# A streaming-encoder block in split float32: seven products for twelve units of the down product, sums and gate multiplications queued elsewhere, and smaller moves at the beginning and the tail

## The chip, the cores and the metric

One core of a Trainium2 chip runs the whole block in one launch. The metric is the device time in microseconds (us), the median of repeated runs. The engines are named as in the profile: PE (TensorE, matmuls and transposes), PEld (its weight loads), DVE (VectorE), ACT (ScalarE), POOL (GpSimd) and SP (SyncE, which issues nearly all DMAs). A trace comes from one profiled execution; its span runs from the first to the last instruction.

## What is computed

One layer on a batch of 256 tokens of 2048 channels in float32, with 256 memory tokens:

```python
def swiglu(h, w_gate, w_up, w_down):
    return (jax.nn.silu(h @ w_gate) * (h @ w_up)) @ w_down

x = x + 0.5 * swiglu(rms_norm(x, ffn1_norm), ffn1_w_gate, ffn1_w_up, ffn1_w_down)
h = rms_norm(x, mix_norm)
u, q, k, v, g, a_lr = split(h @ w_in)
x = x + concatenate([pool_mixer(u), gla_mixer(q, k, v, g, a_lr)]) @ w_out
x = x + mem_cross_attention(rms_norm(x, xattn_norm), rms_norm(mem, mem_norm), w_q, w_kv, w_o)
x = x + 0.5 * swiglu(rms_norm(x, ffn2_norm), ffn2_w_gate, ffn2_w_up, ffn2_w_down)
out = rms_norm(x, final_norm)
```

The hidden width of both FFNs is 5632, eleven pieces of 512. The pool mixer has four channel groups with trailing means; the GLA mixer is gated linear attention with four heads in chunks of 64 tokens.

## The kernel before

**Numbers.** Every float32 operand is split into a high part and a low part of the type fp32r: the high part is a cast (ACT, `wh`, `xh`, line 228), the low part a subtraction (DVE, `wl`, `xl`, line 229). A product is three matmuls: high by high, high by low, low by high (`products`, which ends in line 307).

**Units.** The weights come in units of 1 MB, two k-tiles of 128 rows by 1024 columns. A unit is loaded by SP (`raw`, three buffers, three units ahead), split into `wh` and `wl` (three buffers; two units ahead, one ahead for the first four) and used by 24 matmuls of 128x512 in `block_t` (line 307): 2 k-tiles x 2 halves of the columns (j) x 2 halves of the tokens (h) x 3. `block_a` and `block_b` are other forms for `w_in`, `w_kv` and such.

**Seven products.** In `block_s` (gate and up, lines 401 to 460) the units of `PAIRS` (0, 2, 4) are done by Winograd's form of Strassen's scheme: the 2x2 block product (2 token halves by 2 k-tiles, 2 k-tiles by 2 column halves) takes seven block products for eight, 21 matmuls for 24. It needs sums of the weight blocks (`add_weights`, lines 363, 366 and 367, into `T`), split again (`wh<-T`, `wl<-T`, and `xh`, `xl` for the three blocks used as they are), sums of the activations (`part_sums`, into `xe`, lines 346 to 357), and at the end sums of the PSUM banks (`combine`, lines 443 to 448, into `sg`; `join`, line 452). Two PSUM tiles, `parts`, take four of the seven products, two others, `ps`, the result itself.

**Order.** `Stream` collects units and operations. `st.op(f, after=n)` puts an operation behind n more units; the program order that this gives is then arranged by a scheduler, which fixes one order for each engine. PSUM has four tiles of two banks, handed out as they come free.

**FFN.** The hidden pieces come in three parts, `FF_PARTS = ((0, 4), (4, 4), (8, 3))`. In each part, gate and up of two pieces at a time: `ev_gate` applies SiLU with the row factor `Rcol` (line 676, ACT), `ev_up` multiplies by up and `Rcol` (line 681, DVE, into `sg`), `turn` transposes the result on PE (line 691, `ph`) and splits it into `ys` (lines 234 and 235). The third part ends with one piece whose gate and up make one block. Then the down product (`into_x`, two column blocks b of `block_t`) adds to x by `residual` (line 608). Both down products of the third part and all other products into x keep this form; the last one of FFN 2 is `down_end`.

**Beginning.** `turn_gains` transposes a tile of the norms' gains (line 539, `pgain`), `x_chunk` transposes x by PE (line 575, `px`), scales it by the gains and splits it into `xs` (lines 210 and 211); `x_squares` and `finish_norm` make `Rcol` (lines 186 to 198) while the first gate runs, since the row factor is applied to its results.

**Mixer.** `pool_unit` makes four groups (`pp`, line 805) that `pool_out` evicts; `scores` and `attend` (`po`, line 954) handle the four GLA heads, in two pairs b, behind the units of v.

**Tail.** In `down_end` the last unit of every column block leaves its second token half for `second_half`: x is updated (line 1188), squared (line 1191), the row factor made (lines 1196 and 186 to 198), and eight output pieces multiplied (lines 1203 to 1209) and written (line 1210).

Of the kernel before, what the change touches and what calls it, by code (L numbers as in the profile page):

```python
# [14 lines left out]
P = 128  # L15
D = 2048
# [76 lines left out]
def build(ctx, tc, I, out):  # L93
# [87 lines left out]


# [43 lines left out]

    def split_weights(hi, lo, src):
        in_turn("scalar", lambda: nc.scalar.copy(hi, src))  # L228
        in_turn("vector", lambda: nc.vector.tensor_tensor(  # L229
            out=lo, in0=src, in1=f32(hi), op=ALU.subtract  # L230
        ))
# [8 lines left out]
    def row_squares(src, c):  # L240

        for h in range(2):
            j = tmp.tile([P, S], F32, tag="j", name=uid("j"), bufs=2)
            nc.scalar.activation(j, src[h], AF.Square, accum_out=ss[:, h, c : c + 1])
# [96 lines left out]
    def part_sums(act, ext, i, g):  # L341

        t = scope["pool"].tile([P, 4 * NB], F32, tag="T", name=uid("T"))
        a = t[:, :NB].rearrange("p (k s) -> p k s", k=2)
        e = t[:, NB : 2 * NB].rearrange("p (n s) -> p n s", n=4)
        nc.vector.tensor_tensor(
            out=a, in0=f32(act[:, 2 * g : 2 * g + 2, 0, :]), in1=f32(act[:, 2 * g : 2 * g + 2, 1, :]),
            op=ALU.add,
        )
        a11, a21, a12, a22 = (a[:, k, h * P : (h + 1) * P] for k in range(2) for h in range(2))  # L350
        nc.vector.tensor_tensor(out=e[:, 3], in0=a11, in1=a21, op=ALU.subtract)
# [33 lines left out]
    def seven(banks, act, ext, i, g, first, later, weights):  # L385
# [3 lines left out]
        n4, n1, s2, s3 = ([ext[:, i, p, n] for p in range(2)] for n in range(4))  # L389
# [6 lines left out]
        order = ("P1", "P7", "P5", "P6", "P2", "P3", "P4") if first else (  # L396
            "P1", "P2", "P3", "P7", "P5", "P6", "P4")
        for n in order:
            (a, b), wh, wl = table[n]
            for j, (x, w) in enumerate(((a, wh), (a, wl), (b, wh))):  # L400
                nc.tensor.matmul(  # L401
                    banks[n], x, w, start=first and j == 0,
                    stop=not later and n in ("P1", "P5", "P6", "P7") and j == 2,
                )

    def block_s(srcs, act, ext, pairs, evict, delays=(0, 0)):

        held, n = {}, len(srcs)

        def open_banks():  # L410
            a, b, c, d = (ptile(uid("pt")) for _ in range(4))
            held["ps"] = (d, c)
            held["parts"] = (a, b)
            held["banks"] = {
                "P1": a[:, 0], "P6": a[:, 1], "P7": b[:, 0], "P5": b[:, 1],
                "P2": c[:, 0], "P4": c[:, 1], "P3": d[:, 0],
            }

        def unit_s(g):
            def fn(weights):  # L420
                if g == pairs[0]:
                    open_banks()
                seven(held["banks"], act, ext, pairs.index(g), g, g == pairs[0], g != pairs[-1],
                      weights)
            return fn

        def unit_p(g):
            def fn(wh, wl):
                wh, wl = (w.rearrange("p (k j n) -> p k j n", j=2, n=NB) for w in (wh, wl))
                for j in (1, 0):  # L430
                    for h in range(2):
                        for kk in range(2):

                            fresh = (j, h) == (0, 1) and g == min(set(range(n)) - set(pairs)) and kk == 0
                            products(held["ps"][j][:, h, :], act, 2 * g + kk, h, wh[:, kk, j],
                                     wl[:, kk, j], fresh, g == n - 1 and kk == 1)
            return fn

        def combine():
# [8 lines left out]
            nc.vector.tensor_tensor(out=e[:, 3], in0=b[:, 1], in1=e[:, 1], op=ALU.add)  # L448

        def join(j):  # L450
            e = held["e"][:, 0:2] if j else held["e"][:, 2:4]
# [5 lines left out]
        for g, src in enumerate(srcs):  # L457
            if g in pairs:
                st.unit(src, unit_s(g), split_seven, add_weights)
                if g == pairs[-1]:  # L460
                    st.op(combine)
            else:
                st.unit(src, unit_p(g))
        for j in (1, 0):
            st.op(lambda j=j: join(j), delays[j])
# [65 lines left out]
    def gain_columns(names, queue):  # L531
        t = rows["gain"] = scope["pool"].tile([P, P], F32, tag="gain", name=uid("gain"), bufs=2)
        nc.vector.memset(t, 0.0)
# [3 lines left out]
    def turn_gains(lo, hi):  # L537
        ps = ptile(uid("pgain"))
        nc.tensor.transpose(ps[:, 0, :P], rows["gain"], ident)
        nc.vector.tensor_copy(gains[:, lo:hi], ps[:, 0, lo:hi])  # L540
# [63 lines left out]
    def residual(scale, b):  # L604

        def evict(j, ps):
# [4 lines left out]
            if j:  # L611
                store_x(b)
        return evict

    def fold(c, gain):
# [10 lines left out]
        for h in range(2):  # L626
            q = tmp.tile([P, NB], F32, tag="j", name=uid("j"), bufs=2)
            nc.scalar.activation(q, x[:, h], AF.Square, accum_out=ss[:, h, c : c + 1])

    def into_x(w, act, scale, gain=None, k0=0, nk=KT, spread_too=True, src=None):  # L630

        for b in range(2):
            st.op(lambda b=b: fetch_x(b, src), 2)
            block_t(wwide(w, b * 2 * NB, k0, nk), act, residual(scale, b))
# [10 lines left out]
    PAIRS = (0, 2, 4)  # L645

    def pair_sums(g, delay):
        def f():
            if g == PAIRS[0]:
                rows["xe"] = scope["pool"].tile(  # L650
# [659 lines left out]
```

## Time and profile before

| | us |
|---|---|
| median of 3 runs | 2133.31 (2133.0 to 2134.68) |
| profiled execution | 2133.11 |
| its span | 2131.2 |
| PE busy | 2111.3 |
| DVE busy | 1427.7 |
| ACT busy | 1008.0 |
| matmuls and transposes on PE | 10032 |
| mean TensorE clock granted | 0.999 of full |

The page of the profile has a part with busy time by engine, one with the span in 40 slices, the DMA queues, the chain of work that ended last (followed back from the last instruction), and the costliest groups of instructions. In a group's row stands: line, engine, operation, output <- inputs by the program's names, shape, count | busy time, mean ns of one | idle time of the engine ahead of them and what ended it. The chain can be cut to a window; its rows are start, length, and what. A timeline's rows are start, busy time and the instruction, with the engine's idle time before it in brackets. The view of stretches gives for each stretch its length and the busy time (and instructions) of PE, PEld, DVE, ACT and POOL, then the clock, the busy share of the DMA engines and GB/s.

### The profile page before, as it was taken

How to read it: one execution, taken by the hardware profiler on the slowest of the kernel's cores; microseconds unless marked ns; L12 is line 12 of the kernel's file. 1: busy time of each engine (PE TensorE's matmuls, PEld its weight loads, DVE VectorE, ACT ScalarE, POOL GpSimd, SP SyncE). 2: the span in 40 equal slices, each digit the busy share in tenths (PEclk: the TensorE clock that was granted, in tenths of full speed). 3: DMA queues.
4: the chain of work that ended last, by engine and by line, in shares of the span. 5: the costliest groups of instructions: out<-in, count | busy, mean ns of one | idle time of the engine just before them, and what ended most of it. 6: DMA issues, size and time to landing. Idle time of an engine off the chain costs nothing.

```text
span 2131.2 us, 24070 instructions
## 1 busy us (share of the span) xinstructions
PE 2111.3 (99%) x10032; PEld 1768.5 (83%) x10032; DVE 1427.7 (67%) x1189; ACT 1008.0 (47%) x890; POOL 14.2 (1%) x41
## 2 busy tenths in 40 slices
PE   9999999999999999999999999999999999999998
PEld 7878888888888888888888888888888888888886
DVE  8876588856864576565666454567874888658744
ACT  7554354534534545455445443445443455434433
POOL 0000000000000000000000000000000000000001
PEclk9999999999999999999999999999999999999999
DMA  7556665566656655557654555666576665766663
GB/s 277 197 189 234 224 221 195 186 233 226 227 178 234 221 162 180 167 185 278 222 190 161 167 169 171 195 207 207 175 247 217 214 209 175 249 212 223 221 217 119
DMA packets 143316, 435.91 MB, mean 205 GB/s; under 512 B 9828, under 2 KB 13000, under 8 KB 142824
## 3 DMA queue, kind: packets, MB, share of 16 engines
q1 hardware_dynamic: 143176, 434.38, 60.5%
q8 instruction: 78, 1.28, 0.2%
q14 instruction: 30, 0.25, 0.0%
q10 hardware_dynamic: 32, 0.01, 0.0%
HBM read 417.58 MB, written 16.78 MB: 204 GB/s over the span
## 4 chain that ended last, share of the span: by engine, by line
PE 98%; DVE 1%; issue 0%; ACT 0%; DMA 0%; SPq 0%; DVEq 0%; ACTq 0%
PE pt L307 58%; PE pa L292 15%; PE pt L401 12%; PE pb L307 6%; PE pe L307 3%; PE ph L691 1%; PE pl L1084 1%; PE pv L1119 1%; PE px L621 0%; DVE wl L229 0%; ACT wh L228 0%; DMA x<-in_x 0%; PE px L575 0%; PE po L954 0%; PE pa L832 0%
## 5 line engine op out<-in xcount | busy, mean ns | idle before, releaser
L229 DVE TENSOR_TENSOR wl<-raw,wh 128x2048 fp32r<-128x2048 f32 (+2 forms) x328 | 740.2, 2258 | 544.5 <-ACT wh L228 543.9
L228 ACT CAST wh<-raw 128x2048 fp32r<-128x2048 f32 (+2 forms) x328 | 618.5, 1886 | 721.7 <-PE pt L307 490.5
L307 PE MATMUL pt<-wh,xs 128*128 128x512 f32 x1952 | 618.6, 390 | 0.0
L307 PE MATMUL pt<-wh,ys 128*128 128x512 f32 x1728 | 534.7, 389 | 0.0
L307 PEld LDWEIGHTS pt<-wh,xs 128*128 128x128 f32 x1952 | 366.6, 188 | 75.7
L307 PE MATMUL pt<-wl,xs 128*128 128x512 f32 x976 | 380.8, 390 | 0.0
L307 PEld LDWEIGHTS pt<-wh,ys 128*128 128x128 f32 x1728 | 324.1, 188 | 67.0
L307 PE MATMUL pt<-wl,ys 128*128 128x512 f32 x864 | 336.3, 389 | 0.0
L292 PE MATMUL pa<-xs,wh 128*128 128x512 f32 x896 | 317.1, 398 | 2.1 <-DVE t L266 1.7
L292 PE MATMUL pa<-xs,wl 128*128 128x256 f32 x896 | 248.8, 281 | 0.0
L307 PEld LDWEIGHTS pt<-wl,xs 128*128 128x128 f32 x976 | 183.5, 188 | 37.9
L292 PEld LDWEIGHTS pa<-xs,wh 128*128 128x128 f32 x896 | 167.7, 188 | 41.2 <-issue 2.0
L307 PEld LDWEIGHTS pt<-wl,ys 128*128 128x128 f32 x864 | 162.2, 188 | 33.5
L292 PEld LDWEIGHTS pa<-xs,wl 128*128 128x128 f32 x896 | 169.2, 189 | 1.6 <-issue 0.2
L228 ACT CAST wh<-T 128x2048 fp32r<-128x2048 f32 x54 | 103.3, 1912 | 135.6 <-DVE T L367 93.3
L229 DVE TENSOR_TENSOR wl<-T,wh 128x2048 fp32r<-128x2048 f32 x54 | 123.6, 2288 | 65.3 <-ACT wh L228 65.3
L307 PE MATMUL pb<-wh,xs 128*128 128x512 f32 x384 | 121.7, 392 | 0.5 <-DVE ys L211 0.5
L401 PE MATMUL pt<-wh,xe 128*128 128x512 f32 x324 | 108.7, 389 | 0.0
L229 DVE TENSOR_TENSOR xl<-raw,xh 128x1536 fp32r<-128x1536 f32 x54 | 94.5, 1750 | 2.7 <-ACT xh L228 2.7
L228 ACT CAST xh<-raw 128x1536 fp32r<-128x1536 f32 x54 | 79.9, 1479 | 28.9 <-PE pt L401 28.8
L307 PEld LDWEIGHTS pb<-wh,xs 128*128 128x128 f32 x384 | 72.0, 188 | 15.6 <-DVE ys L211 0.7
L401 PE MATMUL pt<-xh,xs 128*128 128x512 f32 x216 | 78.6, 389 | 1.7 <-DVE sg L452 1.7
(203 smaller groups left out, 1666.3 us busy)
## 6 DMA issues: line engine op xcount, KB each, us to landing
raw<-in_ffn_w_down SPq DMA_DIRECT2D x88, 1024.0 KB, 5.5
raw<-in_ffn_w_up SPq DMA_DIRECT2D x80, 1024.0 KB, 5.0
raw<-in_ffn_w_gate SPq DMA_DIRECT2D x77, 1024.0 KB, 5.0
raw<-in_w_in SPq DMA_DIRECT2D x32, 1024.0 KB, 5.2
raw<-in_xattn_w_kv SPq DMA_DIRECT2D x32, 1024.0 KB, 5.2
raw<-in_w_out SPq DMA_DIRECT2D x16, 1024.0 KB, 6.2
raw<-in_xattn_w_q SPq DMA_DIRECT2D x16, 1024.0 KB, 5.2
raw<-in_xattn_w_o SPq DMA_DIRECT2D x16, 1024.0 KB, 5.6
```

Of the source, the lines that this page charges most:

```text
L228: in_turn("scalar", lambda: nc.scalar.copy(hi, src))
L229: in_turn("vector", lambda: nc.vector.tensor_tensor(out=lo, in0=src, in1=f32(hi), op=ALU.subtract))
L292: nc.tensor.matmul(o, w, x, start=k == 0 and i == 0, stop=last and i == 1)
L307: nc.tensor.matmul(ps, a, w, start=first and i == 0, stop=last and i == 2)
L401: nc.tensor.matmul(banks[n], x, w, start=first and j == 0, stop=not later and n in ("P1", "P5", "P6", "P7") and j == 2,)
L691: nc.tensor.transpose(v[:, i, h * P : (h + 1) * P], g[:, h, i * P : (i + 1) * P], ident)
L1084: nc.tensor.matmul(ps[:, t, :M], ys[:, 4 * h + d, a, tok], xa["K"][:, d, b, :], start=i == 0, stop=i == 11,)
L1119: nc.tensor.matmul(ps[:, d, :S], xa["V"][:, m, a, col], xa["PT"][:, m, b, :], start=i == 0, stop=i == 5,)
```

## The change

1. **Down products of the parts 0 and 1** (both FFNs): `into_x` uses `block_s` for them. In the first column block unit 0 is a seven-product unit, in the second units 0 and 4, in the orders of `Y_ORDER`. `block_s` can take its units in any order, opens the banks of the four part products at the first seven-product unit, and adds the combined parts to x in `merge` as soon as they are there, the whole banks at the end (`residual`).
2. **Sums** of activations become a class. For `ys` (`over`) the fourth sum takes the place of the block of `ys` that no product needs; the others go to a tile `ye`. The temporary is one shared tile of 128x512, `j`.
3. **Gate multiplications** (`late_up`) are queued two units later, or at once ahead of a down product, and behind the latest weight splits (`behind_weights`); turns two or three units later than before in some places.
4. **Sums of FFN 1's activations**: points 5, 6, 7 in place of 5, 5, 5; FFN 2's: 5, 6, 7 in place of 3, 4, 5.
5. **Beginning**: twelve spare transposes, 16 rows of gains transposed rather than 128 with a memset, x chunks 3 to 7 one unit earlier.
6. **Mixer**: two pool groups share one PSUM tile; scores and what follows for the second pair of heads one unit earlier.
7. **Tail**: all matmuls ahead of the row factors, an order of evictions written out, row factor 0 interleaved with the first update, output pieces in halves.

The diff, cut to its core:

```diff
+    def spare_transposes(n):
+        ps = ptile(uid("pwarm"))
+        for _ in range(n):
+            nc.tensor.transpose(ps[:, 0, :P], ident, ident)
...
+    def behind_weights(f):
+        with tc.issue_after(latest["vector"].ins), tc.issue_after(latest["scalar"].ins):
+            f()
...
-    def part_sums(act, ext, i, g):
-        t = scope["pool"].tile([P, 4 * NB], F32, tag="T", name=uid("T"))
-        a = t[:, :NB].rearrange("p (k s) -> p k s", k=2)
-        e = t[:, NB : 2 * NB].rearrange("p (n s) -> p n s", n=4)
-        nc.vector.tensor_tensor(
-            out=a, in0=f32(act[:, 2 * g : 2 * g + 2, 0, :]), in1=f32(act[:, 2 * g : 2 * g + 2, 1, :]),
-            op=ALU.add,
-        )
-        a11, a21, a12, a22 = (a[:, k, h * P : (h + 1) * P] for k in range(2) for h in range(2))
-        nc.vector.tensor_tensor(out=e[:, 3], in0=a11, in1=a21, op=ALU.subtract)
-        nc.vector.tensor_tensor(out=e[:, 1], in0=a22, in1=a21, op=ALU.subtract)
-        nc.vector.scalar_tensor_tensor(
-            out=e[:, 2], in0=e[:, 1], scalar=-1.0, in1=a11, op0=ALU.mult, op1=ALU.subtract
-        )
-        nc.vector.tensor_tensor(out=e[:, 0], in0=a12, in1=e[:, 2], op=ALU.add)
-        split(ext[:, i, 0], ext[:, i, 1], e)
+    def jtile():
+        return tmp.tile([P, NB], F32, tag="j", name=uid("j"))
+    class Sums:
+        def __init__(self, name, act, pairs, over):
+            self.name, self.act, self.pairs, self.over = name, act, pairs, over
+        def make(self, g):
+            act, i = self.act, self.pairs.index(g)
+            n = 3 if self.over else 4
+            if i == 0:
+                self.tile = scope["pool"].tile(
+                    [P, len(self.pairs), 2, n, P], F32R, tag=self.name, name=uid(self.name)
+                )
+            a, k = jtile(), slice(2 * g, 2 * g + 2)
+            nc.vector.tensor_tensor(
+                out=a.rearrange("p (k s) -> p k s", k=2), in0=f32(act[:, k, 0, :]),
+                in1=f32(act[:, k, 1, :]), op=ALU.add,
+            )
+            a = a.rearrange("p (n s) -> p n s", n=4)
+            p11, p21, p12, p22 = (a[:, m] for m in range(4))
+            nc.vector.tensor_tensor(out=p11, in0=p11, in1=p21, op=ALU.subtract)
+            nc.vector.tensor_tensor(out=p21, in0=p22, in1=p21, op=ALU.subtract)
+            nc.vector.scalar_tensor_tensor(
+                out=p22, in0=p11, scalar=-1.0, in1=p22, op0=ALU.mult, op1=ALU.subtract
+            )
+            nc.vector.tensor_tensor(out=p12, in0=p12, in1=p22, op=ALU.add)
+            split(self.tile[:, i, 0], self.tile[:, i, 1], a[:, 4 - n :])
+            if self.over:
+                split(act[:, 2 * g, 0, P:], act[:, 2 * g, 1, P:], p11)
+        def parts(self, g):
+            i, n = self.pairs.index(g), 3 if self.over else 4
+            t = [[self.tile[:, i, p, m] for p in range(2)] for m in range(n)]
+            return [[self.act[:, 2 * g, p, P:] for p in range(2)]] + t if self.over else t
...
-    def block_s(srcs, act, ext, pairs, evict, delays=(0, 0)):
-        held, n = {}, len(srcs)
-        def open_banks():
-            a, b, c, d = (ptile(uid("pt")) for _ in range(4))
-            held["ps"] = (d, c)
-            held["parts"] = (a, b)
-            held["banks"] = {
-                "P1": a[:, 0], "P6": a[:, 1], "P7": b[:, 0], "P5": b[:, 1],
-                "P2": c[:, 0], "P4": c[:, 1], "P3": d[:, 0],
-            }
+    def block_s(srcs, act, sums, order, evict, merge=None, sevens=None):
+        sevens = [g for g in order if g in (sevens or sums.pairs)]
+        held, seen = {"banks": {}}, set()
+        def banks(*names):
+            t = ptile(uid("pt"))
+            for i, n in enumerate(names):
+                held["banks"][n] = t[:, i]
+            return t
+        def open_whole():
+            if "ps" not in held:
+                c = banks("P2", "P4")
+                held["ps"] = (banks("P3", "P0"), c)
+        def open_parts():
+            held["parts"] = (banks("P1", "P6"), banks("P7", "P5"))
...
+            if merge is not None:
+                merge(e[:, 2:4], e[:, 0:2])
         def join(j):
+            if merge is not None:
+                evict(j, held["ps"][j])
...
-        for g, src in enumerate(srcs):
+        for g in order:
+            if g in sevens:
+                st.unit(srcs[g], unit_s(g), split_seven, add_weights)
...
     def turn_gains(lo, hi):
         ps = ptile(uid("pgain"))
-        nc.tensor.transpose(ps[:, 0, :P], rows["gain"], ident)
-        nc.vector.tensor_copy(gains[:, lo:hi], ps[:, 0, lo:hi])
+        n = hi if lo == 0 else P
+        nc.tensor.transpose(ps[:, 0, :n], rows["gain"][:n, :], ident[:n, :n])
+        copied = nc.vector.tensor_copy(gains[:, lo:hi], ps[:, 0, lo:hi])
+        if lo == 0:
+            latest["vector"] = copied
...
+    def early_parts(scale, b):
+        def merge(minus, plus):
+            for j, e, s in ((1, plus, scale), (0, minus, -scale)):
+                x = x_cols((2 * b + j) * NB, NB)
+                nc.vector.scalar_tensor_tensor(
+                    out=x, in0=e, scalar=s, in1=x, op0=ALU.mult, op1=ALU.add
+                )
+        return merge
...
+            if sums is None:
+                block_t(cols, act, residual(scale, b))
+            else:
+                block_s(cols, act, sums, Y_ORDER[b], residual(scale, b, 0), early_parts(scale, b),
+                        Y_SEVEN[b])
...
+    PAIRS, Y_PAIRS = (0, 2, 4), (0, 4)
+    Y_ORDER = ((1, 2, 3, 4, 0, 5, 6, 7), (1, 2, 0, 3, 4, 5, 6, 7))
+    Y_SEVEN = ((0,), (0, 4))
+    CLEAR = PAIRS[-1] + 2
...
+        def late_up(held, j, c):
+            behind_weights(lambda: ev_up(j, c, held))
...
+        for i, g in enumerate(PAIRS):
+            st.op(lambda g=g: x_sums.make(g), 5 + i)
         for lo, n in FF_PARTS:
+            whole = n == KT // 4
...
+                held, up = {}, {}
+                into_down = whole and b
+                block_s(wwide(wu, n0), xs, x_sums, range(8), up.__setitem__)
                 st.op(lambda held=held: held.update(gate))
-                wait = PAIRS[-1] + 2 if b + 2 < n - 1 else 1
+                for j in (1, 0):
+                    st.op(lambda j=j, held=held, up=up: late_up(held, j, up[j]),
+                          0 if into_down else 2)
+                wait = CLEAR if b + 2 < n - 1 else 1 if into_down else 4
...
+            if whole:
+                for g, after in zip(Y_PAIRS, (2, 4)):
+                    st.op(lambda g=g: behind_weights(lambda: y_sums.make(g)), after)
+            down(wd, 4 * lo, 4 * n, lo + n == FF // NB, y_sums if whole else None)
+    st.op(lambda: spare_transposes(12))
     st.op(lambda: turn_gains(0, G_MIX))
-    for c in range(8):
-        st.op(lambda c=c: x_chunk(c), c - 1)
+    st.op(lambda: x_chunk(0))
+    for c in range(1, 8):
+        st.op(lambda c=c: x_chunk(c), c - 1 if c < 3 else c - 2)
...
-    for g in PAIRS:
-        pair_sums(g, 5)
...
-            ps = ptile(uid("pp"))
+            if g % 2 == 0:
+                two = ptile(uid("pp"))
+            ps = two[:, g % 2, :].rearrange("p (a b) -> p a b", a=2)
...
-            st.op(lambda h=h: scores(h), 1 + i)
-            st.op(lambda h=h: attend(h), 2 + i)
-            st.op(lambda h=h: head_squares(h), 2 + i)
+            at = 1 + i - b
+            st.op(lambda h=h: scores(h), at)
+            st.op(lambda h=h: attend(h), at + 1)
+            st.op(lambda h=h: head_squares(h), at + 1)
...
         def second_half():
-            row_factor(0)
-            finish(0, 0, nc.scalar)
-            finish(0, 3)
-            mm(0, nk - 2, 1, *kept[0])
-            finish(0, 1, nc.scalar)
-            finish(0, 2)
-            mm(1, nk - 2, 1, *kept[1])
+            act, dve, half = nc.scalar, nc.vector, NB // 2
+            for b in range(2):
+                mm(b, nk - 2, 1, *kept[b])
+            row_factor(0, lambda: in_order(update(0, 1)))
+            in_order(square(0, 1))
+            weigh(0, 1)
+            finish(act, 0, 0)
+            in_order(update(1, 1))
+            in_order(square(1, 1))
+            weigh(1, 1)
+            finish(act, 0, 1, 0, half)
+            in_order(update(2, 1))
+            in_order(square(2, 1))
+            in_order(update(3, 1))
+            in_order(square(3, 1))
+            finish(dve, 0, 2)
+            finish(dve, 0, 3, 0, half)
+            finish(act, 0, 1, half, NB)
             row_factor(1)
-            for c in range(4):
-                finish(1, c, nc.scalar if c == 1 else None)
+            finish(dve, 1, 2)
+            finish(act, 1, 0)
+            finish(dve, 1, 3)
+            finish(act, 1, 1)
+            finish(dve, 0, 3, half, NB)
...
-    for n, g in enumerate(PAIRS):
-        pair_sums(g, 3 + n)
```

More of the change, by code (lines that the diff above doesn't have):

```diff
@@ L383, in split_seven, with seven @@
         return [parts], None
-    def seven(banks, act, ext, i, g, first, later, weights):
+    def seven(banks, act, sums, g, fresh, ends, weights):
         th, tl, rh, rl = weights
@@ L388, in seven @@
         a11, a12, a22 = ([act[:, k, p, t] for p in range(2)] for k, t in ((k0, lo), (k1, lo), (k1, hi)))
-        n4, n1, s2, s3 = ([ext[:, i, p, n] for p in range(2)] for n in range(4))
+        s3, n1, n4, s2 = sums.parts(g)
         table = {
@@ L431, in fn @@
                     for h in range(2):
+                        n = names[j, h]
                         for kk in range(2):
-                            fresh = (j, h) == (0, 1) and g == min(set(range(n)) - set(pairs)) and kk == 0
-                            products(held["ps"][j][:, h, :], act, 2 * g + kk, h, wh[:, kk, j],
-                                     wl[:, kk, j], fresh, g == n - 1 and kk == 1)
+                            products(held["banks"][n], act, 2 * g + kk, h, wh[:, kk, j],
+                                     wl[:, kk, j], n not in seen and kk == 0,
+                                     g == order[-1] and kk == 1)
+                        seen.add(n)
             return fn
@@ L1145, in last_gain, with down_last @@
         nc.sync.dma_start(fin["gB"], I["final_norm"].partition_broadcast(P))
-    def down_last(wd, k0, nk, last):
+    def down_last(wd, k0, nk, last, sums):
         if last:
@@ L1150, in down_last @@
         else:
[L1151 removed]
+            into_x(wd, ys, 0.5, None, k0, nk, sums=sums)
     def down_end(wd, k0, nk):
```

146 lines of the change are left out of this document (80 added, 66 removed).

## The prediction, made before the result was known

> **What bounds the kernel now.** I read the page first: the busy shares, then the chain that ended last.
>
> ```profile
> span 2131.2 us, 24070 instructions
> PE 2111.3 (99%) x10032; PEld 1768.5 (83%) x10032; DVE 1427.7 (67%) x1189; ACT 1008.0 (47%) x890; POOL 14.2 (1%) x41
> PE 98%; DVE 1%; issue 0%; ACT 0%; DMA 0%; SPq 0%; DVEq 0%; ACTq 0%
> L307 PE MATMUL pt<-wh,ys 128*128 128x512 f32 x1728 | 534.7, 389 | 0.0
> ```
>
> TensorE (PE) is busy 99% of the span and holds 98% of the chain, so a matmul removed is time removed, as long as nothing that feeds PE becomes late. VectorE (DVE) is next with 67%. What one matmul is worth is not the 389 ns of the last row: matmuls overlap. The spacing is read from the chain cut to the first 320 us, where whole units stand as pieces without a gap (columns: start, length, what).
>
> ```profile
> 69.23 5.44 PE pt L307 x24
> 74.67 4.76 PE pt L401 x21
> 79.44 16.32 PE pt L307 x72
> ...
> 190.57 1.75 PE ph L691 x16
> 192.32 79.15 PE pt L307 x349
> ```
>
> A plain unit of 24 matmuls takes 5.44 us, a seven-product unit of 21 takes 4.76: 0.2267 us per matmul, 0.68 us saved per unit. At 389 ns it would seem 1.17 us. Where PE waits at all, the view of its waits tells (total, times, longest):
>
> ```profile
> PE pgain L539 <- DMA gain<-in_ffn_norm: 4.1, 1, 4.1
> PE pt L401 <- DVE sg L452: 1.7, 1, 1.7
> PE pa L292 <- DVE t L266: 1.7, 1, 1.7
> PE po L954 <- DVE ST L947: 1.0, 1, 1.0
> PE pp L805 <- DVE k L266: 0.6, 1, 0.6
> PE pb L307 <- DVE ys L211: 0.5, 1, 0.5
> ```
>
> Apart from the beginning, that is 5.5 us in all; the rest streams.
>
> **Seven products in the down product.** Part 0's and part 1's downs each have two column blocks of 8 units; the change makes 1 of 8 and then 2 of 8 seven-product units. 3 units x 2 downs x 2 FFNs = 12 units. PE: 12 x 3 = 36 matmuls fewer, 36 x 0.2267 = **-8.16 us**. The order of instructions confirms the count: 6096 plain matmuls for 6384, and 252 more of the seven-product line.
>
> The price is on DVE (grouped lines of the whole span; the last view is cut to the first whole down, 182.2 to 271.4 us):
>
> ```profile
> L229 DVE TENSOR_TENSOR wl<-raw,wh 128x2048 fp32r<-128x2048 f32 x320 | 732.6, 2290 | 542.7 <-ACT wh L228 542.2
> L229 DVE TENSOR_TENSOR xl<-raw,xh 128x1536 fp32r<-128x1536 f32 x54 | 94.5, 1750 | 2.7 <-ACT xh L228 2.7
> L363 DVE TENSOR_TENSOR T<-raw 128x1024 f32<-128x1024 f32 x54 | 65.9, 1221 | 2.3 <-DMA raw<-in_ffn_w_up 1.2
> L366 DVE TENSOR_TENSOR T<-T,raw 128x512 f32<-128x512 f32 x54 | 37.0, 686 | 0.7
> L608 DVE SCALAR_TENSOR_TENSOR x<-pt,x 128x1024 f32<-128x1024 f32 x28 | 34.0, 1218 | 0.6
> L681 DVE SCALAR_TENSOR_TENSOR sg<-sg,Rcol,sg 128x512 f32<-128x512 f32 x40 | 27.6, 744 | 0.0
> L235 DVE TENSOR_TENSOR ys<-ph,ys 128x1024 fp32r<-128x1024 f32 x22 | 26.2, 1217 | 2.4 <-ACT ys L234 2.4
> L351 DVE TENSOR_TENSOR T<-T 128x128 f32<-128x128 f32 x6 | 1.7, 286 | 0.1
> ```
>
> ```profile
> 182.20:271.40 89.20, 89.20 (x403) 74.06 (x403) 53.41 (x34) 35.31 (x20) 0.00 (x0) 1.00 0.64 224
> ```
>
> Per seven-product unit DVE gets the weight sums and a second low part: 1.22 + 2 x 0.69 + 1.75 = 4.35, three times 13.0. Two sums of activations: 0.69 + 4 x 0.29 and the low parts 0.69 + 0.29, nearly 3 each, say 6. Two combinations of banks (1.22 + 0.69 + 0.69) and merges into x (2.4 to 2.5): 5 each, 10. Together about 29 us more. In that window DVE is busy 53.4 of 89.2 us (its fourth column), so 82.5 of 87.2: it fits, tightly, so the place matters and not the sum. The first of the three is the tightest. From the end of the up product PE has two turns (1.75) and four plain units (21.8) before it needs the low parts of unit 0: 23.5 us. In DVE's order there stand behind the end of the up product: two joins 2.44, four gate multiplications 2.98, two low parts 4.58, weight sums 2.60, the second low part 1.75, two splits of ys 2.44, the sums' first steps and small splits 2.1, the low part itself 2.29: 21.2. The first join can start half a unit before the end, the cast of the summed weights adds a gap of half a us: ready at about 21, so 2.5 us ahead. For the next two units and the whole-bank eviction behind them I get margins of 1 to 2 us in the same way. I take 0 for waits here; the other end is half a unit per down, 2.7 us, four times: +11.
>
> **Gate multiplications** (L681, now L749) go behind two weight splits. The work is the same, 4 x 0.74 us per pair, and their results are wanted only by turns which are queued two units or more later; cover: these two units, 10.9 us on PE. In the down the multiplications stay ahead of the weights. 0. Without cover each us late would be a us for the turn.
>
> **Activation sums of FFN 1 moved.** Before, one call at one point made them; now pairs 0, 2, 4 are made at points 5, 6, 7, with one shared temporary. In the order of instructions the last pairs and the steps of the first row factor Rcol (finish_norm) slip behind the seven-product units' low parts: the last reciprocal stands behind the third unit's first weight sum. Rows around it before:
>
> ```profile
> 47.59 0.16 DVE L198 RECIPROCAL Rcol<-chain 128x2 f32<-128x2 f32 x1
> ...
> 53.52 2.42 ACT L676 ACTIVATE sg<-pt,Rcol 128x512 f32<-128x512 f32 x4
> ...
> 57.77 2.29 DVE L229 TENSOR_TENSOR wl<-T,wh 128x2048 fp32r<-128x2048 f32 x1 [2.95 <-ACT wh L228]
> 60.10 1.22 DVE L363 TENSOR_TENSOR T<-raw 128x1024 f32<-128x1024 f32 x1
> ```
>
> Rcol is ready at 47.75, the SiLU of the first gate starts at 53.5 when its matmuls end, and frees two bank pairs in time. In the new order: the last cast of that stretch waits for the buffer that unit 7 holds, to 54.35, and ends at 56.3; low part 58.5; split of a sum 59.2; weight sum 60.4; Rcol 60.5; two SiLUs (2.42 for four, 1.2) 61.7. PE by then has done the first unit's 12 matmuls into its own banks and, pulled forward, 12 of the next one's, and stands at about 59.6 before a bank that comes free at 61.7: a new wait of about **+2.1 us** at "pt <- sg". Bounds: 0 if the scheduler's order leaves Rcol as early as now, +4 if the weights behind are late as well.
>
> **Start.** Twelve transposes of the identity are put ahead, the gain is a 16-row transpose, ScalarE (ACT) casts two pieces of the first weight before the first xs.
>
> ```profile
> 4.13 0.45 PE L539 MATMUL pgain<-ident,gain 128*128 128x128 f32 x1 [4.13 <-DMA gain<-in_ffn_norm]
> ...
> 5.76 1.12 PE L575 MATMUL px<-ident,x 128*128 128x128 f32 x4 [0.34 <-DMA x<-in_x]
> 6.53 0.78 PE L307 MATMUL pt<-wh,xs 128*128 128x512 f32 x1
> ...
> 8.39 0.58 PE L307 MATMUL pt<-wl,xs 128*128 128x512 f32 x1
> ...
> 9.27 0.40 PE L307 MATMUL pt<-wl,xs 128*128 128x512 f32 x1
> ```
>
> ```profile
> 6.88 3.71 PE pt L307 x12
> ```
>
> ```profile
> 6.68 0.62 ACT L228 CAST wh<-raw 128x512 fp32r<-128x512 f32 x1 [0.74 <-DMA raw<-in_ffn_w_gate]
> ```
>
> The second piece arrives at 6.68 as before, is cast to 7.3, and the first xs follows, about 7.7: the first main matmul is 1.2 us later. But the first twelve end at 10.59 now, 3.71 us for what 12 x 0.2267 = 2.72 would do: at the full rate a start at 7.87 would end there too. If the transposes bring PE to the full rate by 7.7, this gains 0.2: **-0.2 us**, bounds -0.5 (x chunks come a unit earlier) and +1.2 (none of it).
>
> The Trainium skill, page "TensorE: Matmul & The Clock Gate", section "Part 4: PE-mode transpose", says that the full clock does not engage for transposes, which do not count as a busy PE; by it the twelve warm nothing. This speaks against the change; the trace does not settle it, as slow transposes and slow products follow one another here; by it the start would cost about 1 us.
>
> **Pool.** Two groups share a PSUM tile, so the pool unit takes 2 tiles and not 4, and PE need not wait for a free one: the waits at pp and pb, 0.6 + 0.5, **-1.1 us**. Bounds -1.1 and 0 (the evictions they wait for are there still).
>
> **Scores** of the second head pair one unit earlier: in the order of PE they still follow their q directly, so the waits at po and pa stay. 0; bounds -2.7 (both gone) and +0.5.
>
> **Tail.** The last update no longer waits behind two multiplications by Rcol, but one more output piece follows the last row factor.
>
> ```profile
> 2121.10 6.54 SPq L1210 DMA_DIRECT2D out<-x  x8
> ...
> 2121.28 0.39 PE L307 MATMUL pe<-wh,ys 128*128 128x512 f32 x1
> ...
> 2122.40 0.68 DVE L1188 SCALAR_TENSOR_TENSOR x<-pe,x 128x512 f32<-128x512 f32 x1
> ...
> 2125.05 0.16 DVE L198 RECIPROCAL Rcol<-chain 128x1 f32<-128x1 f32 x1
> ```
>
> The last matmul starts at 2121.28, the update could start 0.7 earlier than 2122.40, Rcol be ready at 2124.5. But five issues of 0.4 to 0.5 us each follow it instead of four, and the last issue sets the landing: 0. Bounds -0.7 and +0.5.
>
> **Sum.** -8.16 + 2.1 - 0.2 - 1.1 = -7.4. The profiled execution took 2133.11 us (span 2131.2 and 1.9 around it), 0.2 under the median of 2133.31: 2125.7 by its own time, **2125.9 us** against the median.
>
> **The rivals.**
> (A) Rcol is in time: the new wait of 2.1 does not come; 2123.8. For it: the gate's banks were free with 2 us to spare. Against: the order of instructions puts five DVE steps ahead.
> (B) Slower: in the downs the chain of turn, split of ys, sums, splits of sums misses its margin of 2.5 us at the first unit and of 1 to 2 at the next two. DVE at 95% there has little to catch up with, and the next low parts are late in turn. It costs what the lateness exceeds; from 7.4 / 4 = 1.85 us of wait per whole down the change is worth nothing, and at 1.3 us for each of the 12 units, 15.6, it is 2141.5. Against: DVE is idle for 36 us of that window today, and in its order the new steps stand ahead of plain low parts that have a unit to spare.
> (C) It does not do what it says: PE's matmuls go, but half of the saving comes back as short waits, 1 us per down, because the seven-product units need low parts 0.68 us sooner than plain ones: 2129.9. For it: same tightness.
> (D) Only 512-wide products bring PE to the full rate: a matmul takes 0.78 and 0.58 us at 6.53 and 8.39, and 0.40 at 9.27, so the full rate came some 2 to 2.5 us after the first main matmul. Two us at about half the rate lose 1 us: 2126.9. For it: the products right after the transposes (the last at 5.76) are slow still. Against: those transposes were few, and PE waited between them. The skill's rule named above is this case.
>
> **How the numbers follow.** Forecast 0.45, A 0.15, B 0.12, C 0.13, D 0.15. A measurement here can tell 0.2%, 4.3 us, from no change: faster is below 2129.0, slower above 2137.6. Forecast, A and D are faster (0.75), C within, B mostly above (0.10): 0.75, 0.15, 0.10. The range starts below A, at 2122.5 (A with the earlier scores in part), takes in the forecast's bounds and C: up to 2131.
>
> **What would show it.** 36 matmuls fewer of width 512, twelve pieces of 4.76 us in the downs, no wait of PE on wl or ye there, at least 1 us of DVE idle ahead of each sum; a wait of about 2 us on the SiLU near 60 us; the waits at pp and pb gone, those at po and pa unchanged; first main matmul near 7.7 with 0.23 us spacing; from the last matmul to the end some 10 us, as now (2121.3 to 2131.2). It is wrong if the downs show waits above 2 us each, or if the sum of the waits does not carry the difference.

## The result, and the profile after

The changed kernel takes 2138.65 us (median of 16 runs, 2135.61 to 2141.65), the kernel before 2134.42 us (16 runs, 2132.25 to 2135.35) on the same chips: ratio 1.0022, 95% interval 1.0014 to 1.0030. It is slower by 4.2 us, where 7.4 us less were forecast. The page of the changed kernel, first its span, the busy time of the engines and the chain that ended last:

```profile
span 2135.5 us, 24222 instructions
PE 2110.5 (99%) x10008; PEld 1764.6 (83%) x10008; DVE 1528.0 (72%) x1332; ACT 1036.1 (49%) x928; POOL 14.0 (1%) x40
...
PE 94%; DVE 3%; ACT 1%; issue 1%; DMA 0%; SPq 0%; DVEq 0%; ACTq 0%
```

PE has 24 instructions fewer: 36 matmuls less and 12 transposes more. Its share of the chain fell from 98% to 94%: DVE and ACT now end waits. Which, the view of PE's waits shows (total, times, longest):

```profile
PE pa L303 <- DVE t L277: 2.6, 1, 2.6
PE pt L435 <- ACT wh L239: 2.6, 2, 1.3
PE pt L435 <- DVE sg L505: 2.1, 2, 1.7
PE pt L318 <- ACT wh L239: 1.7, 2, 0.8
...
PE pt L318 <- ACT xs L216: 1.4, 1, 1.4
PE pt L435 <- ACT sg L741: 1.1, 1, 1.1
PE pt L435 <- DVE xl L240: 0.8, 1, 0.8
PE pt L435 <- DVE wl L240: 0.7, 1, 0.7
PE po L1035 <- DVE ST L1028: 0.6, 1, 0.6
```

The starts of PE's first matmul of each stage, read from both timelines, put the difference of the two spans (4.3 us) in its places:

| stage | before, us | after, us | difference |
|---|---|---|---|
| beginning to the first down (its first matmul at) | 182.47 | 185.28 | +2.81 |
| the four changed downs | 355.29 | 347.14 | -8.15 |
| part 1's gates and ups, FFN 1 | 167.74 | 174.20 | +6.46 |
| part 1's gates and ups, FFN 2 | 167.74 | 170.79 | +3.05 |
| pool unit | 7.25 | 5.74 | -1.51 |
| mixer from v to the output product | 104.12 | 106.12 | +2.00 |
| all the rest, the tail among it | | | -0.4 |

Of the first row, 0.2 us is the beginning and 2.6 us the first gate and up: the 201st main matmul (128x512 into `pt`) starts at 55.93 us before and 56.16 after, the 231st at 62.73 and 65.56.

The downs do what was forecast, to 0.01 us. The chain that ended last in the changed kernel, cut to the first down from 195 us on, shows it streaming without a gap, with its three pieces of 4.76 us:

```profile
195.13 13.84 PE pt L318 x61
208.97 4.76 PE pt L435 x21
213.73 27.20 PE pt L318 x120
240.93 4.76 PE pt L435 x21
245.69 5.44 PE pt L318 x24
251.13 4.76 PE pt L435 x21
```

What they win is lost again right behind them, in gate and up of part 1, where the diff changes little. The view of stretches, for that stage of FFN 1 (start:end, length, then busy time and instructions of PE, PEld, DVE, ACT and POOL, the clock granted, DMA share, GB/s), before:

```profile
271.31:439.05 167.74, 167.74 (x750) 139.04 (x749) 138.46 (x100) 84.13 (x56) 0.00 (x0) 1.00 0.60 207
```

and after, with the 3.3 us that follow its longest waits as a second stretch:

```profile
272.05:446.25 174.20, 170.83 (x749) 139.88 (x748) 140.81 (x103) 83.14 (x56) 0.00 (x0) 0.99 0.58 199
...
381.40:384.70 3.30, 3.30 (x9) 2.55 (x10) 3.30 (x2) 1.36 (x2) 0.00 (x0) 0.52 0.13 20
```

DVE has the same work there, 138 and 141 us, and is idle for 33 of the 174: it isn't full. But its idle time has another cause. The grouped lines of that stage, DVE alone, before:

```profile
L229 DVE TENSOR_TENSOR wl<-raw,wh 128x2048 fp32r<-128x2048 f32 x21 | 48.0, 2288 | 15.9 <-ACT wh L228 15.8
...
L452 DVE TENSOR_TENSOR sg<-pt,sg 128x1024 f32<-128x1024 f32 x7 | 8.5, 1217 | 0.0
```

and after:

```profile
L240 DVE TENSOR_TENSOR wl<-raw,wh 128x2048 fp32r<-128x2048 f32 x21 | 47.8, 2286 | 7.2 <-ACT wh L239 7.2
...
L505 DVE TENSOR_TENSOR sg<-pt,sg 128x1024 f32<-128x1024 f32 x7 | 8.5, 1220 | 6.5 <-PE pt L318 6.5
```

The join (L452, now L505) never waited for PE; now it waits for 6.5 us, twice 3.25, with the next block's low parts queued behind it. The order of DVE has changed. Before, the low part of the next gate's first seven-product unit (`wl<-T`) is done ahead of the join:

```profile
346.12 2.29 DVE L229 TENSOR_TENSOR wl<-T,wh 128x2048 fp32r<-128x2048 f32 x1
...
353.83 1.22 DVE L452 TENSOR_TENSOR sg<-pt,sg 128x1024 f32<-128x1024 f32 x1
```

and after the change it follows the join, though the cast that it needs is done at 351.3:

```profile
352.49 1.22 DVE L505 TENSOR_TENSOR sg<-pt,sg 128x1024 f32<-128x1024 f32 x1 [3.25 <-PE pt L318]
353.63 2.28 DVE L240 TENSOR_TENSOR wl<-T,wh 128x2048 fp32r<-128x2048 f32 x1
```

The chain that ended last in the changed kernel, from there on (start, length, what):

```profile
352.49 0.04 DVE sg L505
...
353.63 1.61 DVE wl L240
...
355.83 2.28 DVE wl L240
...
360.91 1.15 DVE T L397
...
363.61 1.92 ACT wh L239
...
370.05 2.65 DVE sg L749 x4
...
376.14 0.70 DVE T L401
...
378.75 1.91 ACT wh L239
...
381.22 3.91 PE pt L435 x9
```

From 352 to 381 us the path is DVE and ACT, not PE: the join is done as soon as PE's banks are complete, the low parts of the first seven-product unit follow it and are just in time, the second unit's are, and the third's (weight sums to 376.8, cast, low part) are not: PE waits 1.3 and 0.8 us at 377 to 381. Nine matmuls then take 3.91 us: after these waits the clock is granted at half, as the 0.52 of the stretch above shows. The second late join, at 399.5 us, is followed by waits of 0.8 and 0.4 us at 406 to 408.

So a lead of one unit is lost, and it is lost before the join. Counted from the stage's first matmul, the low part of the first gate's second seven-product unit ends at 5.2 us before and at 9.8 after the change, that of its third at 16.6 and 20.5, and the one shown ahead of the join and behind it at 77.1 and 83.9.

### The profile page after: what moved, and what is told of

Read it like the earlier page. It is cut to its first block, busy times and chain, and to the rows that moved or that the text cites. A ratio compares the mean times of both kernels' runs of the same rounds, so it can differ in the third digit from the quotient of the medians.

```text
span 2135.5 us, 24222 instructions
## 1 busy us (share of the span) xinstructions
PE 2110.5 (99%) x10008; PEld 1764.6 (83%) x10008; DVE 1528.0 (72%) x1332; ACT 1036.1 (49%) x928; POOL 14.0 (1%) x40
## 4 chain that ended last, share of the span: by engine, by line
PE 94%; DVE 3%; ACT 1%; issue 1%; DMA 0%; SPq 0%; DVEq 0%; ACTq 0%
PE pt L318 53%; PE pa L303 15%; PE pt L435 13%; PE pb L318 6%; PE pe L318 3%; DVE wl L240 1%; PE ph L759 1%; ACT wh L239 1%; DVE xl L240 1%; PE pl L1166 1%; PE pv L1201 1%; PE px L688 0%; DVE T L397 0%; PE pp L886 0%; DVE sg L749 0%
## 5 line engine op out<-in xcount | busy, mean ns | idle before, releaser
L240 DVE TENSOR_TENSOR wl<-raw,wh 128x2048 fp32r<-128x2048 f32 (+2 forms) x316 | 712.3, 2256 | 399.3 <-ACT wh L239 398.8
L239 ACT CAST wh<-raw 128x2048 fp32r<-128x2048 f32 (+2 forms) x316 | 594.9, 1884 | 561.3 <-PE pt L318 338.0
L318 PE MATMUL pt<-wh,ys 128*128 128x512 f32 x1536 | 477.4, 390 | 0.0
L318 PEld LDWEIGHTS pt<-wh,ys 128*128 128x128 f32 x1536 | 288.0, 188 | 59.6
L318 PE MATMUL pt<-wl,ys 128*128 128x512 f32 x768 | 298.9, 389 | 0.0
L239 ACT CAST wh<-T 128x2048 fp32r<-128x2048 f32 x66 | 126.2, 1912 | 246.9 <-DVE T L401 218.7
L240 DVE TENSOR_TENSOR wl<-T,wh 128x2048 fp32r<-128x2048 f32 x66 | 151.2, 2290 | 94.0 <-ACT wh L239 94.0
L318 PEld LDWEIGHTS pt<-wl,ys 128*128 128x128 f32 x768 | 144.2, 188 | 29.6
L240 DVE TENSOR_TENSOR xl<-raw,xh 128x1536 fp32r<-128x1536 f32 x66 | 115.5, 1750 | 1.2 <-ACT xh L239 1.2
L239 ACT CAST xh<-raw 128x1536 fp32r<-128x1536 f32 x66 | 97.6, 1478 | 15.1 <-PE pt L435 7.9
```

What stands on the lines that cost most here:

```text
L240: in_turn("vector", lambda: nc.vector.tensor_tensor(out=lo, in0=src, in1=f32(hi), op=ALU.subtract))
L318: nc.tensor.matmul(ps, a, w, start=first and i == 0, stop=last and i == 2)
```

## The experiments

Line numbers are those of each kernel's own profile. The ratio is to the kernel before, run on the same chip, with its 95% interval.

**1. The seven products taken out again.**

```diff
-            down(wd, 4 * lo, 4 * n, lo + n == FF // NB, y_sums if whole else None)
+            down(wd, 4 * lo, 4 * n, lo + n == FF // NB, None)
```

(and the `y_sums` operations left out).

> All of the change but the seven products: the down products of parts 0 and 1 are plain again and their sums are gone (36 matmuls more). Theory 'lost lead': the downs' extra work leaves DVE one unit less ahead, the order of part 1's gate and up then puts a join in front of the next block's low part, and PE waits at 377 and 405 us (FFN 1) and at 1779 us (FFN 2). Then here part 1's gate and up of FFN 1 take 167.7 us as before (174.2 in the changed kernel) and of FFN 2 3.0 less than in the changed kernel; the downs give back 4 x 2.04, and the time is 8.16 - 9.5 = 1.3 us below the changed kernel, about 2137. Rival 'late multiplications' (four in one piece behind two low parts hold DVE in part 1): the waits stay, and the time is 8.2 above the changed kernel, about 2147.

2138.34 us, ratio 1.0017 (1.0007 to 1.0027). Part 1's gates and ups in both FFNs, in the view of stretches:

```profile
274.25:441.99 167.74, 167.74 (x749) 139.04 (x748) 138.45 (x100) 84.14 (x56) 0.00 (x0) 1.00 0.62 207
1672.07:1839.81 167.74, 167.74 (x750) 139.04 (x748) 138.97 (x100) 84.22 (x56) 0.00 (x0) 1.00 0.62 207
```

Exactly as before the change, with the late multiplications still in, and the low parts named above end at 5.2, 16.6 and 77.1 us again. So the downs' extra work causes the waits 100 us later. By the two profiles these waits, with the halved clock after one of them, cost 9.5 us, more than the 8.15 that the downs save. In the time the two cancel: 2138.34 us here and 2138.65 in the changed kernel, and a difference of 1.3 us, as forecast, can't be told from none at this spread.

**2. Multiplications not queued late.** `ev_up` as the eviction of the up block, turns at the old points.

```diff
-                block_s(wwide(wu, n0), xs, x_sums, range(8), up.__setitem__)
+                block_s(wwide(wu, n0), xs, x_sums, range(8), ev_up)
```

> All of the change, but the gate multiplications run at the join as before and the turns come as before. 'Lost lead': part 1's gate and up stay above 172 us in FFN 1, since the join still stands ahead of the low part; the time is within 2 us of the changed kernel. 'Late multiplications': they fall to 167.7, the waits at 377, 405 and 1779 us are gone, and the time is about 9 us lower, 2129.

2139.62 us, ratio 1.0029 (1.0019 to 1.0038). Part 1 takes 172.5 us in FFN 1 and 174.5 in FFN 2: the waits stay and only move (368, 382, 405 us); in FFN 2 eight matmuls from 1807.6 us on are 0.43 us apart as well, half the rate. The late multiplications aren't needed for the waits: the rival falls.

**3. Sums of xs at their old points.**

```diff
-            st.op(lambda g=g: x_sums.make(g), 5 + i)
+            st.op(lambda g=g: x_sums.make(g), 5)
```

> All of the change, but the three sums of xs are made at points 5, 5, 5 and not at 5, 6, 7 (in both FFNs). Theory 'Rcol late': the row factor is ready some 8 us earlier, the waits at 58 and 61 us (2.1 us) are gone, and the first down starts near 183.2 us and not 185.3; 2 us off the time. Rival 'beginning': the 2.8 us come from the first matmul at 7.75 us; then the down still starts at 185.

2140.00 us, ratio 1.0030 (1.0020 to 1.0039). A miss: the first down starts at 189.3 us, the wait for the SiLU grows from 1.1 to 2.2, and the last reciprocal of Rcol comes at 63.11 (60.74 in the changed kernel): it still stands behind the low part of the second seven-product unit. So the wait doesn't need the moved sums.

**4. Scores at their old points.**

```diff
-            at = 1 + i - b
+            at = 1 + i
```

> All of the change, but scores, attention and squares of the second pair of heads where they were. Theory 'scores': the wait of 2.8 us ahead of the g block becomes 1.9 as before and the half rate after it is gone; from the first matmul of v's block to the output product it takes 104.1 us as before and not 106.1; 2 us off the time. Rival 'shared banks of the pool': the wait stays above 2.5 us, as the pool's two tiles shift what follows.

2137.31 us, ratio 1.0014 (1.0004 to 1.0023). The waits are those of before again (1.6 us ahead of the g block, 1.0 ahead of po, where the changed kernel has 2.6 and 0.6; the expectation counted from start to start), 0.6 us less together. The half rate did not go: it came here too, at 915.5 us after the shorter waits, and from v to the output product it takes 105.5 us. Where that stretch runs at the full rate, it takes 104.7 us with the scores moved (runs 1, 2 and 6) and 104.1 with the old points (before, runs 7 and 8). So 0.6 us of the 2.0 belong to the scores, and some 1.4 to the clock, which this change alone doesn't decide.

**5. No spare transposes.**

```diff
-    st.op(lambda: spare_transposes(12))
```

> All of the change but the twelve spare transposes. In the order of instructions the last reciprocal of Rcol then stands ahead of the low part of the second seven-product unit, as before the change. Theory 'order': the transposes move the row factor, so without them the waits at 58 and 61 us (2.1 us) are gone, and the first down starts near 182.7 us, not 185.3; 2 to 2.5 us off the time. Rival 'moved sums': the row factor is late because its squares and the sums share one temporary, the waits stay. On the clock: if transposes warm PE, the first main matmuls are at half rate here (0.43 us apart) and at full rate more often with them.

2135.02 us, ratio 1.0001 (0.9992 to 1.0011). Timeline of DVE and ACT around the row factor, here:

```profile
48.91 0.16 DVE L204 RECIPROCAL Rcol<-chain 128x2 f32<-128x2 f32 x1
...
57.38 2.29 DVE L240 TENSOR_TENSOR wl<-T,wh 128x2048 fp32r<-128x2048 f32 x1 [0.98 <-ACT wh L239]
```

and in the changed kernel:

```profile
56.72 2.29 DVE L240 TENSOR_TENSOR wl<-T,wh 128x2048 fp32r<-128x2048 f32 x1 [0.52 <-ACT wh L239]
...
60.74 0.15 DVE L204 RECIPROCAL Rcol<-chain 128x2 f32<-128x2 f32 x1
60.93 2.43 ACT L741 ACTIVATE sg<-pt,Rcol 128x512 f32<-128x512 f32 x4 [2.42 <-DVE Rcol L204]
```

Without the transposes Rcol stands 12 us earlier, ahead of that low part, and nothing waits at 58 to 62 us. The first down starts at 182.10 us, 3.18 earlier than in the changed kernel: 2.6 for the waits and the slower matmuls right behind them (the 201st main matmul starts at 55.56 and the 231st at 62.36, in the changed kernel at 56.16 and 65.56), and 0.6 for the beginning. The first main matmul starts at 6.56 and not at 7.75, but the first ones are at half the rate here and at the full rate in the changed kernel's profile, which gives half of the 1.2 us back. Theory 'order' holds; why the scheduler sets Rcol later with the transposes isn't shown.

**6. Two seven-product units in the first gate of part 1.**

```diff
-                    block_s(wwide(wg, n0), xs, x_sums, range(8), lambda j, c: ev_gate(j, c, 0))
+                    block_s(wwide(wg, n0), xs, x_sums, range(8), lambda j, c: ev_gate(j, c, 0),
+                            sevens=(0, 2) if lo == 4 and b == 0 else None)
```

> All of the change, but the first gate of part 1 (both FFNs) has two seven-product units and not three, which costs 2 x 0.68 us on PE and gives DVE 4.35 us there. Theory 'lost lead': in the order of instructions the next low part is ahead of the join again; part 1's gate and up take 167.7 + 0.7 = 168.4 us in FFN 1 (174.2 in the changed kernel), and no waits at 377, 405 or 1779; the time is 9.5 - 1.4 = 8 us below the changed kernel, about 2130.5. Rival: DVE stays too loaded there in any order; then waits of 1 us or more remain in part 1, and the time falls by less than 4 us.

2131.12 us, ratio 0.9979 (0.9970 to 0.9988).

```profile
272.12:440.54 168.42, 168.42 (x752) 139.62 (x751) 137.23 (x99) 82.36 (x55) 0.00 (x0) 1.00 0.61 206
1666.55:1834.97 168.42, 168.42 (x753) 139.62 (x751) 137.24 (x99) 82.36 (x55) 0.00 (x0) 1.00 0.62 206
```

PE is busy through both stages, at the forecast 168.4. Three matmuls more in each FFN buy back 5.8 and 2.4 us. This alone doesn't tell less work from an earlier place; run 9 does.

**7 and 8. All four causes undone**: this gate, the scores at their old points, no spare transposes, and in run 7 the x chunks at their old points too (runs 7 and 10 also leave out the two lines of `turn_gains` that set `latest["vector"]`).

> The change with two seven-product units in the first gate of part 1, the scores where they were, no spare transposes and the x chunks at their old points. If the four causes add (part 1 -8.1, beginning and first up -2.8, scores -0.6, and fewer stretches at half rate), it is 11 to 12 us below the changed kernel: 2127, faster than before by 7 to 8. If one of them only moves its wait elsewhere, it stays above 2130.

> As the run before, but the x chunks stay one unit earlier. 'Chunks harmless': the same time within 0.5 us. 'Chunks cost': earlier chunks put ACT's and DVE's work ahead of the first weight splits, and the first down starts 0.5 us or more later than with the old points.

Run 7: 2124.87 us (2124.36 to 2126.31), ratio 0.9955 (0.9942 to 0.9969). Run 8: 2125.18, ratio 0.9955 (0.9942 to 0.9967); its first down starts 0.2 us later, so the chunks do no harm. Run 7 is the fastest kernel here, 10 us under the kernel before on the same chip. It is 13.8 us under the changed kernel, where 11 to 12 were forecast; by the two profiles its beginning and first up give 2.7, part 1 5.8 and 2.4, and the mixer 2.1, as it runs at the full rate there. Its waits of PE on DVE and ACT are those of before without pp and pb:

```profile
PE pt L435 <- DVE sg L505: 1.7, 1, 1.7
PE pa L303 <- DVE t L277: 1.7, 1, 1.7
PE po L1033 <- DVE ST L1026: 1.0, 1, 1.0
```

**9 and 10. The same work in another order**, alone and with the beginning and the scores of run 7 (every gate with three seven-product units):

```diff
-    Y_ORDER = ((1, 2, 3, 4, 0, 5, 6, 7), (1, 2, 0, 3, 4, 5, 6, 7))
+    Y_ORDER = ((1, 2, 3, 4, 0, 5, 6, 7), (0, 4, 1, 2, 3, 5, 6, 7))
```

> The changed kernel with one line other: the second column block of the down products takes its units in the order 0, 4, 1, 2, 3, 5, 6, 7 and not 1, 2, 0, 3, 4, 5, 6, 7. No instruction is added or removed, all twelve units and all gates keep their seven products; only the two seven-product units come first, so five plain ones follow. In the order of instructions the low parts of part 1's first gate then stand ahead of the joins again. Theory 'lost lead' (where DVE's extra work falls decides, not how much): part 1's gate and up take 167.7 us in both FFNs (174.2 and 170.8 in the changed kernel), and the time is 8 to 9.5 us below the changed kernel, about 2130; the two units at the block's beginning may cost up to 1 us per down there. Rival 'load' (DVE has too much to do in down and part 1 together, and the run with two seven-product units helped because it took 4.35 us away): waits of more than 1 us stay in part 1 and the gain is below 3 us.

> This order of the down's units together with the old beginning (no spare transposes, chunks at their old points) and the old place of the scores, with three seven-product units in every gate: the combined run without its 1.36 us of plain units. 'Lost lead': 2124.9 - 2.7 (two FFNs) = 2122 to 2123.5 if the downs have no waits. 'Load': part 1's waits come back and it is 2130 or more.

Run 9: 2134.78 us, ratio 1.0004 (0.9995 to 1.0013); run 10: 2129.25, ratio 0.9979 (0.9970 to 0.9988). The stretches of run 9, first a whole down, then part 1 of FFN 1 and of FFN 2:

```profile
187.74:275.82 88.08, 87.34 (x393) 72.03 (x391) 78.24 (x70) 41.62 (x29) 0.00 (x0) 1.00 0.64 227
275.82:443.56 167.74, 167.74 (x750) 139.08 (x748) 138.47 (x100) 84.15 (x56) 0.00 (x0) 1.00 0.62 207
1673.88:1841.62 167.74, 167.74 (x750) 139.07 (x748) 138.53 (x100) 84.14 (x56) 0.00 (x0) 1.00 0.63 207
```

No instruction is added or taken away, and part 1 is at 167.74 in both FFNs, the join's idle time 0.0 us again. So it is the place of DVE's extra work, not its amount: with the two units at the block's beginning five plain units follow, and the lead is back when the gate begins: the low parts named above end at 5.2, 16.6 and 77.1 us here too. The price is in the down, 88.08 us and not 86.77, 1.3 in each of four (0.9 and 0.3 us lost from start to start, for weights that come late near 241 us): 5.3 of the 9.5. So the time misses the forecast of about 2130. Run 10 is a miss as well, 2129.25 for 2122 to 2123.5: part 1 has no waits, but the downs take 5.4 us more than in run 7, and its beginning and its mixer lose 0.8 and 1.6, with half the rate at 908 us. So run 7's way, two seven-product units fewer, is cheaper.

## Why the prediction was wrong

**Seven products: right on PE, wrong on what follows.** The -8.16 came as -8.15, at 0.68 per unit, and inside the downs the margins held: no wait there. The step that failed is "I take 0 for waits here". The sum has no other term for what DVE's extra work does to PE, so its account ends at the down's edge and does not ask where DVE would regain its lead. It can't soon: in part 1 DVE is busy 138 of 168 us, with in-order waits on casts and joins in the rest, and its low parts of summed weights end 3 to 7 us later than before in the first 84 us. A join that had always found its banks ready then stood in front of low parts that PE needed. In place of the 0 the runs show 6.46 and 3.05 us in part 1, 1.6 of the 6.46 by the halved clock (172.6 us in run 5, where the same waits were followed by the full rate). The amount of work was not the error: 29 us more of DVE per down were said, and the whole span shows 100.3 us more for four downs, 25 each. Rival B had lateness handed on from unit to unit and a price per unit, but placed it in the downs and set its chance at 0.12; rival C, waits inside the downs, did not come.

**The first gate's wait**: size and path nearly right (2.1 us forecast; 0.9 and 1.2 us of waits from start to start, 2.6 with the slower matmuls behind them; Rcol at 60.74 us for 60.5), what put Rcol there wrong. I put it down to the moved sums; run 3 kept the wait with the old points and run 5 lost it with the moved ones. The spare transposes change the order and with it the place of the row factor.

**Beginning**: the first main matmul came at 7.75 us as forecast, but the gain of 0.2 was a loss of 0.2 in the changed kernel's profile, up to the 201st main matmul. That profile is one of the lucky ones: with spare transposes this matmul starts at 56.2 to 58.6 us (seven profiles), without them at 55.6 to 56.8 (five, 55.9 in the kernel before).

**Rival D** has to be told in two halves. Transposes can bring PE to the full rate: in run 2 the last four of x, ahead of any product, are 0.11 us apart, and the first main matmul is fast:

```profile
6.16 0.66 PE L632 MATMUL px<-ident,x 128*128 128x128 f32 x4 [0.85 <-DMA x<-in_x]
7.82 0.50 PE L318 MATMUL pt<-wh,xs 128*128 128x512 f32 x1 [1.00 <-ACT xs L216]
...
9.24 1.05 PE L318 MATMUL pt<-wh,xs 128*128 128x512 f32 x2
```

But the rate fell again from 8.4 to 11.8 us, after PE had waited 0.85 and 1.0 us. In run 3 the same transposes are 0.21 us apart to the end, and the products begin at half the rate:

```profile
5.86 1.11 PE L632 MATMUL px<-ident,x 128*128 128x128 f32 x4 [0.37 <-DMA x<-in_x]
7.57 0.79 PE L318 MATMUL pt<-wh,xs 128*128 128x512 f32 x1 [0.59 <-ACT xs L216]
```

Of the seven profiles with spare transposes three (the changed kernel, runs 1 and 6) run their first main matmuls at the full rate, four have 6 to 11 of them at half, 0.2 us lost each: run 2, which lost the rate, and runs 3, 4 and 9, which had not reached it. In the five profiles without spare transposes the first main matmul is at half the rate each time. The Trainium skill, page "TensorE: Matmul & The Clock Gate", section "Part 4: PE-mode transpose", says that the full clock does not engage for transposes; here the trace shows that it can (0.11 us apart in run 2), though in three of seven profiles 20 transposes of 128x128 were not enough.

**Pool**: -1.5 for -1.1, right. **Scores**: 0 forecast, 0.6 of waits and 1.4 at half rate after them; the bounds (-2.7 to +0.5) leaned to the wrong side. **Gate multiplications and tail**: 0 and 0, right; from the last matmul to the end it is 10.0 us in both kernels (the issues there take 0.33 to 0.45 us each before, not 0.4 to 0.5).

## What to carry to other kernels

When an engine that isn't the bound gets more work in one stage, the account doesn't end with that stage: ask how far ahead of the bound engine it was, in units, and how long the next stages need to regain that lead. A fixed order makes such a loss dear, because one instruction that waits for the bound engine holds up all that this engine will need next; the idle time of the in-order engine, by what ended it, shows it (0.0 us at the join before, 6.5 after). Placing the extra work early, with slack behind it, was worth 4 us here (run 9), and dropping a little of it in the stage that follows 7.5 us (run 6), beside a saving of 8.15.

## What was not expected of the hardware

The clock can fall to half after short waits of PE: 1.3 and 0.8 us within 4 us were enough at 377 to 381 us (granted clock 0.52 for the next 3.3 us), a wait of 2.6 us at 911 (0.50 from 914.2 to 917.4), and in run 4 waits of 1.0 and 1.6 us. Each time it lasts some 3.4 us and costs about half of that again: 1.6 us in part 1 and 1.4 in the mixer. It does not come every time. The waits of 1.3 and 0.8 us come again at 1779 to 1783 us of the same execution and at 374 to 378 in run 5, and the 2.6 us at 909 in run 1, and all three were followed by the full rate. So a wait of such a length can cost more than itself, and not the same in each run. The changed kernel's 16 runs spread over 6.0 us, with a mean granted clock of 0.997 to 0.999 in the nine shortest and 0.995 or 0.996 in the seven longest; the five of run 7 spread over 2.0, all at 0.998.
